# Transposes of a hybrid layer's mixer moved from TensorE to VectorE and DRAM stores

## The chip, the cores and the metric

One core of one Trainium2 chip runs the whole program in one launch. The metric is the device time of that core in microseconds. The kernel before was run three times: 2200.02, 2205.93 and 2200.26, median 2200.26 us. Engines are named as in the profile: PE is TensorE, DVE is VectorE, ACT is ScalarE, POOL is GpSimd, SP is SyncE, which issues nearly all DMA.

## What is computed

Two layers on a sequence of T = 1024 positions and D = 1024 channels, in float32. Layer 0 has a mixer of two parts that share one input projection, layer 1 a gated linear recurrence; a convolutional feed-forward network (FFN) follows each. The mixer of layer 0, cut to its core:

```python
def retention_deltanet_mixer(hn, pos, w_in, conv_w, a_log, dt_bias, out_gain, w_out):
    q_r, k_r, v_r, g_r, q_d, k_d, v_d, g_d, b_d, a_d = jnp.split(hn @ w_in, split_at, axis=-1)
    ...
    y_r = _rms(retention_chunkwise(q_r, k_r, v_r)).reshape(b, t, RET_WIDTH)
    y_r = y_r * jax.nn.silu(g_r.astype(f32))
    qkv = jax.nn.silu(causal_dwconv(jnp.concatenate([q_d, k_d, v_d], axis=-1), conv_w)).astype(f32)
    ...
    q_d = l2norm(q_d.reshape(b, t, GDN_HEADS, GDN_DK))
    k_d = l2norm(k_d.reshape(b, t, GDN_HEADS, GDN_DK))
    ...
    y_d = gated_delta_chunkwise(q_d, k_d, v_d, g, beta)
    y_d = rms_norm(y_d, out_gain) * jax.nn.silu(g_d.astype(f32).reshape(b, t, GDN_HEADS, GDN_DV))
    y = jnp.concatenate([y_r, y_d.reshape(b, t, GDN_WIDTH)], axis=-1).astype(hn.dtype)
    return y @ w_out
```

Both parts have four heads of 128 channels. Retention works on chunks of 128 positions: scores between q and k, a decaying state, and an RMS norm over the 128 channels of each position. The gated delta rule also solves a unit lower triangular system for each chunk, one for each head.

## The kernel before

**Layout.** Activations stand with channels on the 128 partitions and positions along the free axis. A projection of one head is a *unit*: weights of 1024 x 128, two quarters of 128 x 512. For each of the two halves of the sequence (512 positions) eight input tiles are multiplied into one PSUM bank. Float32 accuracy comes from splitting each operand in a high and a low part and doing three matmuls (`mm3`, L319 to L330): high by high, high by low, low by high. A half is therefore 24 matmuls of 128x512, and two halves rotate through a ring of four banks (`pp`); small products use four other banks (`pc`).

**Weights** are streamed in the order that `quarter_order` writes down: SP loads a raw quarter (L260), ACT casts its high part `whi` (L270), DVE subtracts for its low part `wlo` (L271). Six split quarters may be held at once.

**Order of the work.** `_mix0` projects, in turn, the gated-delta k heads (units 20 to 23), its q heads (16 to 19), four gates (12 to 15), its v heads (24 to 27), then for each retention head q, k and v (h, 4 + h, 8 + h) and a last gate. Beside the projections run *lanes*: lists of generators, of which one step is taken every second slot, a slot being one `mm3`. The lane of the gated delta rule holds the chunk matrices (`a_stage`), the triangular solve (`subst`: 31 steps of two DVE instructions, L1271 and L1273, on 32x32 blocks that 128 partitions hold), `merge` (which assembles 128x128 inverses out of blocks with short matmuls, L1305 to L1337), and eight `scan`s over chunks. The lane of retention holds two `ret_half` for each head. `after(n, f)` runs f n slots later, `flush` runs slots until nothing is left. A scheduler then fixes, for each engine, one order of instructions; an engine works through its own in that order and waits where an operand is not there.

**Transposes.** Scans and retention need v, K and k with positions on the partitions, and their outputs with channels on the partitions again. All of this is done by TensorE against an identity, into PSUM, four at a time: outputs in `post` (L1366, then an ACT copy, L1367, and one DMA to `y_dram`), v in `scan` (L1389), K in `scan` (L1397), v and k in `ret_half` (L1459, L1464). The squared norms of the q heads are sums over channels for each position: `qnorm` does them with eight matmuls against a column of ones (L1345), with positions on the partitions.

**Evacuations** from PSUM multiply by the row R of inverse norms (L388 for gates and heads). Gates go through `gate2` (L1105 on ACT, L1106 on DVE), convolved heads through `conv_tail` (L1203 and L1207 on ACT, L1205 and L1208 on DVE). In `a_stage`, L1235, L1236, L1231 and L1242 are DVE steps, L1246 the stores of blocks to `l_dram`; L1308 is one of merge's ACT copies; L1277 is the reordering copy at the solve's end; L1292 loads blocks of `t_dram` for merge.

**FFN.** Its down projection uses a product scheme with seven operands per group of channels. `store_parts` writes the hidden tiles to DRAM, some operands whole (`sf_dram`), some already split in high and low parts (`pf_dram`); `load_set` reads them back, and splits the whole ones on ACT and DVE (L840, L841).

Of the kernel before, what the change touches and what calls it, by code (L numbers as in the profile page):

```python
# [103 lines left out]
class Block:  # L104
# [82 lines left out]
    def quarter_order(self):  # L187
# [3 lines left out]
        for h in range(NH):  # L191
            o += [(("mix_in", i), 2) for i in (h, 4 + h, 8 + h)]
# [567 lines left out]
    def ffn(self, layer, gain):  # L760
# [3 lines left out]
        s_dram = self.tc.dram_tile([2, 4, 4, P, HALF], F32, name=f"sf_dram{layer}")  # L764
# [15 lines left out]
        place = {1: 0, 4: 1, 2: 2, 6: 3}  # L780
        whole = {0: 0, 1: 1, 3: 2, 5: 3}
        room = {}

        def store_parts(p, y, hi):
# [11 lines left out]
            def store_split(o, src, at):  # L796
                A.copy(halves(hi[:, at]), src)  # L797
                V.tensor_tensor(halves(lo[:, at]), src, f32(halves(hi[:, at])), ALU.subtract)
                for e, t in enumerate((hi, lo)):
                    nc.sync.dma_start(p_dram[c, whole[o], k % 4, e], f32(t[:, at]))  # L800
# [22 lines left out]
            store_split(5, v[:, :, 0], slice(HALF, T))  # L823

        def load_set(c, o):

            x = self.operand(o)
            if o in whole:
                for k in range(4):
                    for e in range(2):  # L830
                        nc.sync.dma_start(f32(x[:, :, 4 * e + k, :]), halves(p_dram[c, whole[o], k, e]))
# [120 lines left out]
    def rglru(self, gain):  # L952
# [5 lines left out]

        sm = lambda name: pool.tile([P, 8], F32, name=name)
# [12 lines left out]
        us = pool.tile([P, 8 * HALF], F32, name="us")  # L972
        xs = pool.tile([P, 4 * T], F32R, name="xs")
# [110 lines left out]
    def mix0(self, gain):  # L1084
        tc = self.tc
        self.q_dram = tc.dram_tile([NCH, P, HALF], F32, name="q_dram")
        self.v_dram = tc.dram_tile([NCH, P, HALF], F32, name="v_dram")
# [21 lines left out]
    def _mix0(self, room):  # L1109
# [89 lines left out]
        def conv_tail(kind, h, buf, dst):  # L1199
# [9 lines left out]
            return th  # L1209

# [131 lines left out]
        def qnorm(h, s):  # L1342
            p = self.pc()
            for n in range(NCH):
                PE.matmul(p[:, n:n + 1], s[:, n * P:(n + 1) * P], self.ones, start=True, stop=True)  # L1345

            V.tensor_scalar(irho[:, h * NCH:(h + 1) * NCH], p[:, 0:NCH], 4.0 * EPS, 128.0 * EPS, ALU.add, ALU.mult)

        def normalise(o, eps, ydst, i):
# [12 lines left out]

            def post():
                p = self.pc()
                for h in range(4):
                    PE.transpose(p[:, hs(h)], on[:, hs(h)], self.ident)  # L1366
                A.copy(s, p)  # L1367
                nc.sync.dma_start(ydst, ps4(s) if len(ydst.shape) == 3 else s)
            self.after(8, post)

        def scan(n):
# [4 lines left out]
            nc.sync.dma_start(v, self.v_dram[n])  # L1376
# [6 lines left out]
            yield from range(2)  # L1383
# [3 lines left out]
            pv = self.pc()  # L1387
            for h in range(NH):
                PE.transpose(pv[:, hs(h)], v[:, hs(h)], self.ident)  # L1389
# [3 lines left out]
            yield  # L1393
            if n < NCH - 1:
                p = self.pc()
                for h in range(NH):
                    PE.transpose(p[:, hs(h)], K[h][:, cs], self.ident)  # L1397
                kt = tmp2("kt")
                V.tensor_tensor(ps4(kt), ps4(p), bc_last(cn(ekt), P), ALU.mult)
            s0, s1 = S[n % 2], S[(n + 1) % 2]  # L1400
            if n > 0:
                p = self.pc()
                for h in range(NH):
                    PE.matmul(p[:, hs(h)], K[h][:, cs], s0[:, hs(h)], start=True, stop=True)
                for h in range(NH):
                    V.scalar_tensor_tensor(v[:, hs(h)], p[:, hs(h)], col(ck, h, n), v[:, hs(h)], ALU.mult, ALU.add)
# [22 lines left out]
            normalise(o, cn(irho), self.y_dram[4:8, :, cs].rearrange("h p c -> p h c"), 0)  # L1429


        def rot_head(ti):
# [3 lines left out]
            def evac(n, sl, ps):  # L1436
# [4 lines left out]
                G.tensor_tensor(r[:, sl], r[:, sl], t, ALU.add)  # L1441
            self.project(unit, evac)
# [266 lines left out]
```

## Time and profile before

| What | Value |
|---|---|
| median of three runs | 2200.26 us |
| the profiled execution | 2200.31 us |
| its span in the trace | 2198.5 us |
| PE busy | 2176.4 us (99%) |
| DVE busy | 1696.0 us (77%) |
| ACT busy | 1069.7 us (49%) |
| POOL busy | 80.8 us (4%) |

The span runs from the first to the last instruction of the trace; 1.8 us of the execution's time lie around it. A line of the trace gives a start, a duration, the engine, the line of the program, the operation and its operands by the program's names; in brackets stands the idle time of that engine just before, and what ended it. Matmuls are pipelined, so their durations overlap, and the distance of starts says what one costs. The mixer's projections and lanes take about the first 480 us.

### The profile page before, as it was taken

How to read it: one execution, taken by the hardware profiler on the slowest of the kernel's cores; microseconds unless marked ns; L12 is line 12 of the kernel's file. 1: busy time of each engine (PE TensorE's matmuls, PEld its weight loads, DVE VectorE, ACT ScalarE, POOL GpSimd, SP SyncE). 2: the span in 40 equal slices, each digit the busy share in tenths (PEclk: the TensorE clock that was granted, in tenths of full speed). 3: DMA queues.
4: the chain of work that ended last, by engine and by line, in shares of the span. 5: the costliest groups of instructions: out<-in, count | busy, mean ns of one | idle time of the engine just before them, and what ended most of it. 6: DMA issues, size and time to landing. Idle time of an engine off the chain costs nothing.

```text
span 2198.5 us, 29909 instructions
## 1 busy us (share of the span) xinstructions
PE 2176.4 (99%) x10844; PEld 1819.5 (83%) x10844; DVE 1696.0 (77%) x2576; ACT 1069.7 (49%) x1712; POOL 80.8 (4%) x73
## 2 busy tenths in 40 slices
PE   9999999999999999999999999999999999999998
PEld 8887888887888888887888888888888888878888
DVE  6988766446899988987865677778999889878644
ACT  5334433124565555554323476765655555544321
POOL 0100111200000000000000000000000000000001
PEclk9999999999999999999999999999999999999999
DMA  4243424125234544438546211242245445375542
GB/s 173 81 141 99 128 83 145 57 79 175 63 120 167 179 153 157 163 111 287 197 160 201 82 53 63 85 147 73 101 165 171 148 173 177 115 271 178 190 165 77
DMA packets 203300, 305.34 MB, mean 139 GB/s; under 512 B 31728, under 2 KB 91408, under 8 KB 203152
## 3 DMA queue, kind: packets, MB, share of 16 engines
q1 hardware_dynamic: 202720, 301.85, 40.7%
q8 instruction: 85, 1.39, 0.3%
q10 hardware_dynamic: 432, 1.58, 0.2%
q14 instruction: 63, 0.52, 0.1%
HBM read 212.63 MB, written 90.72 MB: 138 GB/s over the span
## 4 chain that ended last, share of the span: by engine, by line
PE 89%; DMA 4%; DVE 4%; issue 2%; ACT 1%; POOL 1%; SPq 0%; POOLq 0%; DVEq 0%; ACTq 0%
PE ps L328 27%; PE ps L330 27%; PE ps L329 27%; DMA t<-sf_dram 1%; DMA t<-y_dram 1%; PE pc L433 1%; DMA s<-pf_dram 1%; DMA h<-in_xT_dram 0%; DVE wlo L271 0%; PE pc L448 0%; DVE l L1273 0%; DVE l L1271 0%; PE pc L328 0%; PE pc L330 0%; PE pc L329 0%
## 5 line engine op out<-in xcount | busy, mean ns | idle before, releaser
L328 PE MATMUL ps<-s,whi 128*128 128x512 f32 (+1 forms) x2792 | 1091.0, 392 | 3.9 <-ACT s L840 1.8
L329 PE MATMUL ps<-s,whi 128*128 128x512 f32 (+1 forms) x2792 | 1084.5, 388 | 1.0 <-DVE s L841 0.7
L330 PE MATMUL ps<-s,wlo 128*128 128x512 f32 (+1 forms) x2792 | 1083.9, 388 | 0.0
L270 ACT CAST whi<-raw 128x512 fp32r<-128x512 f32 (+1 forms) x612 | 371.5, 613 | 659.1 <-PE ps L329 515.6
L328 PEld LDWEIGHTS ps<-s,whi 128*128 128x128 f32 x2792 | 524.9, 188 | 112.5 <-ACT s L840 3.1
L330 PEld LDWEIGHTS ps<-s,wlo 128*128 128x128 f32 x2792 | 524.7, 188 | 108.1 <-DVE wlo L271 0.3
L329 PEld LDWEIGHTS ps<-s,whi 128*128 128x128 f32 x2792 | 525.2, 188 | 107.3 <-DVE s L841 1.8
L271 DVE TENSOR_TENSOR wlo<-raw,whi 128x512 fp32r<-128x512 f32 (+1 forms) x612 | 412.9, 680 | 60.8 <-ACT whi L270 57.2
L774 DVE SCALAR_TENSOR_TENSOR t<-halo,cols,t 128x1024 f32<-128x1024 f32 x176 | 222.1, 1282 | 4.8 <-ACT t L772 3.5
L747 DVE TENSOR_TENSOR halo<-ps,kept 128x512 f32<-128x512 f32 (+1 forms) x138 | 92.2, 668 | 75.5 <-PE ps L330 74.2
L757 DVE TENSOR_TENSOR h<-ps,h 128x512 f32<-128x512 f32 x112 | 77.4, 691 | 82.2 <-PE ps L330 81.9
L772 ACT ACTIVATE t<-halo,cols 128x1024 f32<-128x1024 f32 x88 | 109.7, 1246 | 16.9 <-DVE halo L747 11.6
L742 ACT COPY kept<-ps 128x512 f32<-128x512 f32 (+1 forms) x138 | 77.0, 558 | 13.3 <-PE ps L330 11.2
L498 DVE TENSOR_TENSOR h<-ps,h 128x512 f32<-128x512 f32 (+1 forms) x72 | 45.3, 631 | 43.3 <-PE ps L330 43.3
L438 POOL TENSOR_TENSOR rtok<-rtok,npow 128x4 f32<-128x4 f32 (+1 forms) x11 | 11.2, 1016 | 1722.3 <-DVE rtok L437 1668.7
L857 DVE TENSOR_TENSOR t<-t 128x1024 f32<-128x1024 f32 x44 | 53.7, 1221 | 0.0
L797 ACT CAST t<-t 128x512 fp32r<-128x512 f32 x64 | 38.1, 620 | 32.0 <-DVE t L857 30.7
L852 ACT ACTIVATE t<-t 128x1024 f32<-128x1024 f32 x44 | 46.8, 1063 | 10.1 <-DVE t L774 10.0
L416 ACT ACTIVATE t<-h 128x512 f32<-128x512 f32 (+1 forms) x49 | 27.2, 562 | 46.3 <-DVE h L498 41.5
L840 ACT CAST s<-t 128x512 fp32r<-128x512 f32 x48 | 29.5, 621 | 38.4 <-DMA t<-sf_dram 34.0
L328 PE MATMUL ps<-s,s 128*128 128x256 f32 (+1 forms) x144 | 46.2, 321 | 0.0
L329 PE MATMUL ps<-s,s 128*128 128x256 f32 (+1 forms) x144 | 45.8, 318 | 0.0
(293 smaller groups left out, 2074.5 us busy)
## 6 DMA issues: line engine op xcount, KB each, us to landing
raw<-in_ffn_up_dram SPq DMA_DIRECT2D x176, 256.0 KB, 2.7
s<-pf_dram SPq DMA_DIRECT2D x128, 256.0 KB, 5.3
pf_dram<-t SPq DMA_DIRECT2D x64, 256.0 KB, 2.6
pf_dram<-lo SPq DMA_DIRECT2D x64, 256.0 KB, 2.5
sf_dram<-t SPq DMA_DIRECT2D x64, 256.0 KB, 2.2
t<-sf_dram SPq DMA_DIRECT2D x64, 256.0 KB, 5.0
raw<-in_ffn_w_dram SPq DMA_DIRECT2D x64, 256.0 KB, 2.9
raw<-in_mix_in_dram SPq DMA_DIRECT2D x62, 256.0 KB, 2.9
```

What stands on the lines that cost most here:

```text
L270: self.nc.scalar.copy(hi[:, 0:w], raw[:, 0:w])
L271: eng.tensor_tensor(lo[:, 0:w], raw[:, 0:w], f32(hi[:, 0:w]), ALU.subtract)
L328: mm(ps, whi, xhi, start=start, stop=False)
L329: mm(ps, whi, xlo, start=False, stop=False)
L330: mm(ps, wlo, xhi, start=False, stop=stop)
L742: A.copy(kept[o], ps)
L747: V.tensor_tensor(dst(i, j), v(ps), v(kept[k]), ALU.add)
L757: V.tensor_tensor(h(*to[o]), ps.rearrange("p (h c) -> p h c", c=256), h(*to[o]), ALU.add)
L772: A.activation(t, buf[:, 2:2 + T], AF.Identity, scale=w(0), bias=self.col(f"ffn_cb{layer}", tile_i))
L774: V.scalar_tensor_tensor(t, buf[:, 2 + j:2 + j + T], w(j), t, ALU.mult, ALU.add)
L852: A.activation(tg, tg, AF.Silu)
L857: V.tensor_tensor(tg, tg, tv, ALU.mult)
```

## The change

**Transposes.** None of the mixer's is left on TensorE. A new helper `store_t` does block transposes on DVE (each 32x32 block of a tile is transposed in its place) and stores the tile in DRAM with four DMAs that put the blocks in their places, in runs of 32 elements (128 bytes). So K goes to `kt_dram`, v to `v_dram`, the retention's k and v to `rt_dram`; scans and retention load them back with positions on the partitions. `post` transposes blocks on DVE and stores with 4 DMAs (scan) or 16 (retention) in the place of one.

**q norms.** Squares are block-transposed, reduced over 32 and block-transposed again on DVE, stored as rows to `qq_dram`, loaded back with positions on the partitions (elements of 4 bytes), and added on POOL.

**Leads.** Stores wait for three slots (`after(3)`), posts for six instead of eight; a scan loads its tiles four steps ahead of its first matmul instead of two; a retention half keeps four states in the place of two and does its state updates ahead of its output; the heads' units come as v, k, q instead of q, k, v.

**FFN.** Operand 5 of the first group is stored whole instead of split, and split on loading, in both layers. In the recurrence two tiles are allocated ahead of the small ones.

```diff
-            o += [(("mix_in", i), 2) for i in (h, 4 + h, 8 + h)]
+            o += [(("mix_in", i), 2) for i in (8 + h, 4 + h, h)]
...
-        place = {1: 0, 4: 1, 2: 2, 6: 3}
-        whole = {0: 0, 1: 1, 3: 2, 5: 3}
+        place = {1: 0, 4: 1, 2: 2, 6: 3, 5: 4}
+
+        whole = [{0: 0, 1: 1, 3: 2}, {0: 0, 1: 1, 3: 2, 5: 3}]
...
-            store_split(5, v[:, :, 0], slice(HALF, T))
+            if 5 in whole[c]:
+                store_split(5, v[:, :, 0], slice(HALF, T))
+            else:
+                nc.sync.dma_start(halves(s_dram[c, place[5], k % 4]), v[:, :, 0])
...
+        def store_t(dst, src, room):
+
+            V.transpose(room, src)
+
+            def out():
+                for a in range(4):
+                    bs = slice(a * 32, (a + 1) * 32)
+                    nc.sync.dma_start(dst[:, bs].rearrange("(b i) j -> i b j", i=32),
+                                      room[bs, :].rearrange("p (b j) -> p b j", j=32))
+            self.after(3, out)
...
-        def qnorm(h, s):
-            p = self.pc()
-            for n in range(NCH):
-                PE.matmul(p[:, n:n + 1], s[:, n * P:(n + 1) * P], self.ones, start=True, stop=True)
-
-            V.tensor_scalar(irho[:, h * NCH:(h + 1) * NCH], p[:, 0:NCH], 4.0 * EPS, 128.0 * EPS, ALU.add, ALU.mult)
+        def qnorm(h, s, room):
+            V.transpose(room, s)
+            V.tensor_reduce(qb, room.rearrange("p (b j) -> p b j", j=32), AX.X, ALU.add)
+            V.transpose(q32, qb)
+            d = self.qq_dram[h]
...
+            self.after(3, out)
+            self.after(8, load)
+            self.after(15, back)
...
             def post():
-                p = self.pc()
-                for h in range(4):
-                    PE.transpose(p[:, hs(h)], on[:, hs(h)], self.ident)
-                A.copy(s, p)
-                nc.sync.dma_start(ydst, ps4(s) if len(ydst.shape) == 3 else s)
-            self.after(8, post)
+                V.transpose(s, on)
+                for a in range(4):
+                    bs = slice(a * 32, (a + 1) * 32)
+                    for d, c in ydst(a):
+                        nc.sync.dma_start(d, s[bs, c].rearrange("p (m j) -> p m j", j=32))
+            self.after(6, post)
...
+            if n < NCH - 1:
+                kt = tmp2("kt")
+                nc.sync.dma_start(kt, self.kt_dram[cs])
...
-            yield from range(2)
+            yield from range(4)
...
-            pv = self.pc()
-            for h in range(NH):
-                PE.transpose(pv[:, hs(h)], v[:, hs(h)], self.ident)
-            V.tensor_tensor(ps4(v), ps4(pv), bc_last(cn(cv), P), ALU.mult)
+            V.tensor_tensor(ps4(v), ps4(v), bc_last(cn(cv), P), ALU.mult)
...
-            self.after(28, lambda h=h, q2=q2: qnorm(h, q2))
+            qnorm(h, q2, blocks())
+            store_t(self.kt_dram[:, hs(h)], K[h], blocks())
...
-            q = rot_head(h)
-            k = rot_head(4 + h)
...
-            self.project(unit, self.evac_r(v))
-            ret += [ret_half(h, i, q, k, v) for i in range(2)]
+            self.project(self.unit("mix_in", 8 + h), evac)
+            k = rot_head(4 + h, self.rt_dram[1, h])
+            q = rot_head(h)
+            ret_load(h)
+            ret += [ret_half(h, i, q, k) for i in range(2)]
```

The orders of the engines change well beyond the edited lines. On DVE before, at the start of the triangular solve (L1271 and L1273): wlo_1386 and wlo_1392 are the low parts of the first v head's weights (unit 24), ps_1301 and ps_1335 the second gate, ps_1396 the first half of the third gate.

```order
L1106 SCALAR_TENSOR_TENSOR t_1206<-t_1284,t_1206 128x1024
L271 TENSOR_TENSOR wlo_1386<-raw_1383,whi_1385 128x512
L388 TENSOR_TENSOR t_1300<-ps_1301,R_97 128x512
L388 TENSOR_TENSOR t_1300<-ps_1335,R_97 128x512
L1271 TENSOR_TENSOR l0_117<-l0_117 128x31
L271 TENSOR_TENSOR wlo_1392<-raw_1389,whi_1391 128x512
L1273 TENSOR_TENSOR l0_117<-l0_117 128x31
L1271 TENSOR_TENSOR l0_117<-l0_117 128x60
L1273 TENSOR_TENSOR l0_117<-l0_117 128x30x2
L1106 SCALAR_TENSOR_TENSOR t_1300<-t_1379,t_1300 128x1024
```

On DVE in the changed kernel, at the start of the solve (now L1291 and L1293): ps_1516 and ps_1550 are the two halves of the fourth and last gate.

```order
L388 TENSOR_TENSOR t_1515<-ps_1516,R_97 128x512
L388 TENSOR_TENSOR t_1515<-ps_1550,R_97 128x512
L1291 TENSOR_TENSOR l0_120<-l0_120 128x31
L1293 TENSOR_TENSOR l0_120<-l0_120 128x31
L1291 TENSOR_TENSOR l0_120<-l0_120 128x60
L1293 TENSOR_TENSOR l0_120<-l0_120 128x30x2
L1291 TENSOR_TENSOR l0_120<-l0_120 128x87
L1293 TENSOR_TENSOR l0_120<-l0_120 128x29x3
```

And on DVE in the changed kernel, where the first block of the solve ends after its twentieth step: wlo_1421 and wlo_1427 are the low parts of unit 24, wlo_1506 the first of unit 25.

```order
L1291 TENSOR_TENSOR l0_120<-l0_120 128x240
L1293 TENSOR_TENSOR l0_120<-l0_120 128x12x20
L1114 SCALAR_TENSOR_TENSOR t_1515<-t_1584,t_1515 128x1024
L271 TENSOR_TENSOR wlo_1421<-raw_1418,whi_1420 128x512
L271 TENSOR_TENSOR wlo_1427<-raw_1424,whi_1426 128x512
L1291 TENSOR_TENSOR l0_120<-l0_120 128x231
L1293 TENSOR_TENSOR l0_120<-l0_120 128x11x21
L1291 TENSOR_TENSOR l0_120<-l0_120 128x220
L271 TENSOR_TENSOR wlo_1506<-raw_1503,whi_1505 128x512
```

The solve moved from behind the second gate to behind the fourth, and the low parts of unit 24 from its first steps to behind its twentieth.

On PE in the changed kernel, where the last gate (ps_1550) ends and unit 24 (ps_1600, ps_1631) begins:

```order
L328 MATMUL ps_1550<-s1_96,whi_1341 128x512
L329 MATMUL ps_1550<-s1_96,whi_1341 128x512
L330 MATMUL ps_1550<-s1_96,wlo_1342 128x512
L328 MATMUL ps_1600<-s1_96,whi_1420 128x512
L329 MATMUL ps_1600<-s1_96,whi_1420 128x512
L328 MATMUL ps_1631<-s1_96,whi_1420 128x512
L330 MATMUL ps_1600<-s1_96,wlo_1421 128x512
L328 MATMUL ps_1600<-s1_96,whi_1420 128x512
```

Unit 24 follows the last gate with nothing between them, and three of its matmuls stand ahead of the first that needs a low part.

On PE in the changed kernel, the last head's merge (L1325 to L1357) and the first scan (L1428 to L1462):

```order
L1334 MATMUL pc_2307<-l0_120 32x32 x7
L1338 MATMUL pc_2308<-l0_120 32x32 x7
L1351 MATMUL pc_2331<-l0_120,h7_95 64x64 x3
L1351 MATMUL pc_2337<-l0_120,h7_95 64x64 x4
L1357 MATMUL pc_2343<-l0_120 64x64 x4
L1357 MATMUL pc_2350<-l0_120 64x64 x4
L1428 MATMUL pc_2487<-l0_120,h0_88 128x128
L1428 MATMUL pc_2487<-l0_120,h1_89 128x128
L1428 MATMUL pc_2487<-l0_120,h2_90 128x128
L1428 MATMUL pc_2487<-l0_120,h3_91 128x128
L1444 MATMUL pc_2502<-l0_120,h4_92 128x128
```

They stand behind each other without wide matmuls between.

On SP in the changed kernel, the stores of the last K head (kt_dram), the load of the solve's blocks (l_dram) and the raw weights of units 24 and 25:

```order
L1266 DMA l_dram_113<-h7_95 32x4x32 x8
L1371 DMA qq_dram_110<-l0_120 128x32
L1227 DMA kt_dram_108<-lo_1235 32x32x32
L1281 DMA l0_120<-l_dram_113 128x1024
L1227 DMA kt_dram_108<-lo_1235 32x32x32 x3
L1375 DMA l0_120<-qq_dram_110 128x8x1 x4
L1616 DMA g_dram_116<-t_1345 128x1024
L260 DMA raw_1418<-in_mix_in_dram 128x512
L260 DMA raw_1424<-in_mix_in_dram 128x512
```

Before, the first raw quarter of unit 24 (raw_1383) stood ahead of all stores to `l_dram`.

More of the change, by code (lines that the diff above doesn't have):

```diff
@@ L763, in ffn @@
         y_dram = self.tc.dram_tile([16, P, T], F32, name=f"yf_dram{layer}")
[L764 removed]
+        s_dram = self.tc.dram_tile([2, 5, 4, P, HALF], F32, name=f"sf_dram{layer}")
         p_dram = self.tc.dram_tile([2, 4, 4, 2, P, HALF], F32, name=f"pf_dram{layer}")
@@ L1456, in ret_half @@
             yield
[L1457 to L1466 removed]
+            vt, kt = rt[i]
+            A.activation(kt, kt, AF.Copy, scale=ktail[:, h:h + 1])
             yield
@@ L1494, in together @@
                 yield from range(2)
+        blocks = lambda: f32(self.parts.tile([P, T], F32R, tag="lo", name="lo"))
+        half = lambda: self.kept.tile([P, HALF], F32, tag="kept", name="kept")
         gdn = self.lane("gdn", 2, 0)
```

113 lines of the change are left out of this document (66 added, 47 removed).

## The prediction

> **What bounds the kernel now.** I read the busy table first, then the chain that ended last, then the table of stretches, and last the rows of the stretch that the change rewrites.
>
> ```profile
> PE 2176.4 (99%) x10844; PEld 1819.5 (83%) x10844; DVE 1696.0 (77%) x2576; ACT 1069.7 (49%) x1712; POOL 80.8 (4%) x73
> PE 89%; DMA 4%; DVE 4%; issue 2%; ACT 1%; POOL 1%; SPq 0%; POOLq 0%; DVEq 0%; ACTq 0%
> ```
>
> TensorE is busy nearly all the time and carries the chain, so a microsecond of TensorE work that disappears is worth a microsecond, as long as the other engines keep up. Whether they do is read by stretch. The columns below are length, then PE, weight load, DVE, ACT and POOL with counts, granted clock, DMA share and GB/s.
>
> ```profile
> 100.00:150.00 50.00, 50.00 (x270) 43.02 (x269) 41.66 (x105) 21.16 (x41) 8.64 (x4) 1.00 0.47 132
> 150.00:200.00 50.00, 49.74 (x274) 40.01 (x272) 45.51 (x95) 15.30 (x23) 0.00 (x0) 1.00 0.36 118
> 240.00:300.00 60.00, 59.79 (x400) 52.84 (x400) 41.54 (x81) 22.89 (x58) 10.73 (x8) 1.00 0.35 101
> 300.00:360.00 60.00, 57.57 (x386) 51.09 (x385) 42.87 (x90) 21.74 (x53) 14.78 (x12) 1.00 0.32 95
> ```
>
> From 100 to 200 us (gated-delta q heads, gates, v heads) VectorE is 83% and 91% busy beside a full TensorE: it has little room. In the scans (240 to 360 us) it is 69% to 71% busy. The next rows show how VectorE stands against TensorE before 200 us: evacuations of projections (L388) and rows of the triangular solve (L1271, L1273).
>
> ```profile
> 140.04 0.69 DVE L388 TENSOR_TENSOR t<-ps,R 128x512 f32<-128x512 f32 x1
> 149.40 0.20 DVE L1271 TENSOR_TENSOR l<-l 128x31 f32<-128x31 f32 x1
> 152.45 0.69 DVE L388 TENSOR_TENSOR t<-ps,R 128x512 f32<-128x512 f32 x1 [0.31 <-PE ps L330]
> 165.12 0.42 DVE L1271 TENSOR_TENSOR l<-l 128x255 f32<-128x255 f32 x1
> 165.58 0.42 DVE L1273 TENSOR_TENSOR l<-l 128x255 f32<-128x255 f32 x1
> 169.15 0.69 DVE L388 TENSOR_TENSOR t<-ps,R 128x512 f32<-128x512 f32 x1
> 180.23 0.69 DVE L388 TENSOR_TENSOR halo<-ps,R 128x512 f32<-128x512 f32 x1
> 162.00 0.39 PE L329 MATMUL ps<-s,whi 128*128 128x512 f32 x1
> 162.22 0.39 PE L330 MATMUL ps<-s,wlo 128*128 128x512 f32 x1
> 162.45 0.39 PE L328 MATMUL ps<-s,whi 128*128 128x512 f32 x1
> ```
>
> I name units g0 to g3 (mix_in 12 to 15, the gates), v0 to v3 (24 to 27) and their halves a and b. Matmuls start 0.22 to 0.23 us apart (162.00, 162.22, 162.45), 0.227 as I take it, so a half of 24 takes 5.44 us. The row at 152.45 waited for TensorE: it evacuates g2a, which so ran from 147.0 to 152.4. g3b ended 16.3 us later, at about 168.8 (evacuated at 169.15), v0b at about 179.6 (evacuated at 180.23). g0a was evacuated only at 140.04, 7 us before TensorE needed its bank again for g2a (the ring has four): VectorE runs late there, but not so late that TensorE waits. The solve's 31 steps run from 149.40 on, with the casts and evacuations of g2 to v1 between them.
>
> **The change part by part.** First the price of what leaves TensorE: the groups, the q norm in the chain, and one group of four transposes with its successor.
>
> ```profile
> L1366 PE MATMUL pc<-ident,l 128*128 128x128 f32 x64 | 9.6, 272 | 0.0
> L1459 PE MATMUL pc<-ident,t 128*128 128x128 f32 x32 | 4.8, 272 | 0.0
> L1464 PE MATMUL pc<-ident,t 128*128 128x128 f32 x32 | 4.8, 273 | 0.0
> L1389 PE MATMUL pc<-ident,l 128*128 128x128 f32 x32 | 4.8, 273 | 0.0
> L1397 PE MATMUL pc<-ident,h 128*128 128x128 f32 x28 | 4.2, 272 | 0.0
> 100.61 1.68 PE pc L1345 x16
> 144.67 1.68 PE pc L1345 x16
> 273.13 0.60 PE L1389 MATMUL pc<-ident,l 128*128 128x128 f32 x4
> 273.49 0.48 PE L328 MATMUL ps<-s,whi 128*128 128x512 f32 x1
> ```
>
> Busy time overlaps, so I price by starts: four transposes hold TensorE for 273.49 − 273.13 = 0.36 us, and the change back to wide matmuls costs 0.09 (0.48 against 0.39). With the 0.09 where nothing small stands beside them: 16 posts 16 × 0.45 = 7.2, scan v 8 × 0.36 = 2.9, scan K 7 × 0.36 = 2.5, retention v and k 8 × 0.81 = 6.5, together 19.1 us. The four q norms are 4 × (1.68 + 0.09) = 7.1 us. In all 26.2 us of TensorE work goes. Of this, 7.1 lies before 150 us, the rest behind 200 us.
>
> What VectorE gets has no row in this trace: 32x32 block transposes of 128x1024 and 128x512. The nearest rows are full-width operations and a reordering copy.
>
> ```profile
> L1208 DVE SCALAR_TENSOR_TENSOR t<-t 128x1024 f32<-128x1024 f32 x8 | 9.8, 1223 | 0.8 <-ACT t L1207 0.8
> L388 DVE TENSOR_TENSOR t<-ps,R 128x512 f32<-128x512 f32 x24 | 16.4, 688 | 13.1 <-PE ps L330 13.0
> 184.72 1.11 DVE L1277 COPY l<-l 128x1024 f32<-128x1024 f32 x1
> 103.19 1.12 DVE L1242 SCALAR_TENSOR_TENSOR h<-pc,l 128x128 f32<-128x128 f32 x4
> ```
>
> I take 1.2 us for 128x1024 and 0.65 for 128x512, and the same 1.2 for the new 128x1024 reduce; the ends I keep are 1.1 and 2.4 (half rate). [...]
>
> *q heads.* Per head a transpose, a reduce and the transpose of K come to VectorE, 3.6 us, plus 0.1. Three heads of this stand ahead of g0a's evacuation: 11.1 us. Of other work, 8 of the steps L1242 (four take 1.12, so 2.2) and two of L1231 (128x512, 0.6 each, as L388 by starts) now stand behind it, and one L1208 (1.1) ahead. Net +8.8 us, so g0a is evacuated at 140.04 + 8.8 = 148.8 if no idle time takes it up. TensorE would have reached g2a at 147.0 − 7.1 = 139.9; it now waits for that bank until 149.4. The 7.1 us of the q norms are lost in this, and g3b ends at 149.4 + 21.8 = 171.2 instead of 168.8.
>
> *The solve.* This is the term that decides. In the new VectorE order the first twenty steps, 40 instructions, stand in one block behind g3b's evacuation, and only then come L1114 and the low parts of v0's weights; before, v0's low parts stood in front of the second and third instruction of the solve. v0 follows g3 directly on TensorE and can do three matmuls without its low part.
>
> ```profile
> L1271 DVE TENSOR_TENSOR l<-l 128x31 f32<-128x31 f32 (+15 forms) x31 | 10.6, 341 | 0.7
> L1273 DVE TENSOR_TENSOR l<-l 128x31 f32<-128x31 f32 (+15 forms) x31 | 10.6, 342 | 0.8
> ```
>
> Their mean is 0.342 us at a mean width of 176 elements. The first twenty steps have a mean width of 192; from 0.20 at 31 and 0.42 at 255 an element is 0.001 us, so 0.36, and starts lie 0.04 further apart than the duration (165.58 − 165.12 = 0.46 against 0.42): 40 × 0.40 = 16.0 us. With the evacuation (0.6), L1114 (1.1) and one cast (0.6) TensorE waits 18.3 us, until 189.5. Of v0's 10.9 us three matmuls (0.7) are done, so v0 ends at 199.7 against 179.6: **+20.1 us**, the q norms' gain included.
>
> *Merges.* The triangular blocks are put together by short matmuls with ACT and VectorE between them:
>
> ```profile
> 235.89 0.26 ACT l L1308
> 237.02 0.35 ACT l L1321
> ```
>
> Before, wide matmuls stand between nearly all of them. In the new order the last head's merge and scan 0 stand without any behind each other, then wide matmuls whose low part is cast behind scan 0's VectorE work. Of five hops at 0.3 to 1 us each I estimate 5 us for that, and 4 for the three heads before, against the 3 they cost now: **+6** (0 to 10).
>
> *Scans and retention.* 19.1 us of TensorE work goes. VectorE gets 16 posts and 16 retention transposes, 32 × 0.65 = 20.8 us over 240 us: 5.2 more per 60, to 80%. ACT loses 16 copies of the posts, 8 of the retention's. I take 2 us of new waits: **−17.1**. The yields that move loads further ahead (four instead of two) hide DMA that does not stop TensorE now.
>
> *Queues.* The new stores and loads add about 280 DMA issues on SyncE, at 0.44 (the l_dram stores, 1.76 for four) to 0.54 us (the t_dram loads, 9.78 for 18) each and so 120 to 150 us, of which some 100 between 240 and 480 us: about half of that queue. Behind them stand weight loads.
>
> ```profile
> 99.13 1.76 SPq L1246 DMA_DIRECT2D l_dram<-h  x4
> 189.96 9.78 SPq L1292 DMA_DIRECT2D l<-t_dram  x18
> l<-t_dram SPq DMA_DIRECT2D x64, 16.0 KB, 1.9
> ```
>
> Transfers of 128-byte runs land in 1.9 us, and raw tiles are loaded ahead, so I take 0. POOL gets 12 tiny operations behind DMA waits; what it does next is needed late, 0.
>
> *FFN operand 5.* In each layer a load phase reads 1 MB less and splits 4 tiles more (each a cast on ACT and a subtraction on VectorE of 128x512).
>
> ```profile
> 1010.00:1050.00 40.00, 38.31 (x160) 29.04 (x159) 26.93 (x41) 17.25 (x29) 0.00 (x0) 1.00 0.92 325
> 1950.00:1990.00 40.00, 38.48 (x158) 30.27 (x157) 26.92 (x41) 17.10 (x29) 0.00 (x0) 0.96 0.90 320
> L840 ACT CAST s<-t 128x512 fp32r<-128x512 f32 x48 | 29.5, 621 | 38.4 <-DMA t<-sf_dram 34.0 <-PE ps L330 3.7
> 1039.17 0.50 PE L328 MATMUL ps<-s,whi 128*128 128x512 f32 x1 [0.55 <-ACT s L840]
> ```
>
> 160 matmuls at 0.227 are 36.3 us of 40: about 3.7 are lost where DMA is 0.92 busy. 1 MB at 325 GB/s is 3.2 us. ACT's splits (0.62 each) wait for the transfers, and TensorE for the splits, which become more, so I take half, **−3.5** for both layers (0 to −6.4).
>
> Sum: +20.1 + 6 − 17.1 − 3.5 = +5.5 us. The profiled run took 2200.31 us (span 2198.5 and 1.8 around it), 0.05 above the median, so the same sum holds: **2205.8 us**. A measurement of this kernel tells about 0.3%, 6.6 us, from no change. By its terms' ends this case reaches from 2194 (bank wait taken up by idle time, merges covered) to 2216.
>
> **The rivals.**
> *VectorE transposes at half rate* (slower). Six of them ahead of g0a and two ahead of g3 add 8 × 1.2 = 9.6 us on an engine that is already the late one; in the scans 20.8 us become 41.6, and VectorE stands at nearly 90%: 4 more. 2205.8 + 13.6 = 2219. It decides from about 1.9 us per 128x1024. The 1.11 us of the reordering copy speaks against it. [...]
>
> *SyncE late* (slower). A retention post now issues 16 stores, 16 × 0.44 = 7.0 us, ahead of a scan's loads and of weights. If two of the eight reach TensorE: 2219. The four yields speak against it.
>
> *Only the block, no lateness* (faster). If idle VectorE time takes up the transposes, g2a starts at 139.9, g3b ends at 161.7, v0 at 190.2: +10.6; with merges covered and no new waits, 10.6 − 19.1 − 3.5 = −12, 2188. For it: 8.3 us idle between 100 and 150. Against: that idle time lies in waits that stay.
>
> *TensorE stays the bound everywhere* (faster). The weights of v0 come in time after all: 2200.3 − 26.2 − 3.5 = 2171. The order speaks against it. That the change does not remove this work is excluded by the order: the transposes are gone from TensorE.
>
> **How the numbers follow.** Forecast 0.45 (0.02 of it faster, 0.24 same, 0.19 slower), half rate 0.17, SyncE 0.07, only the block 0.21 (0.04 same), TensorE-bound 0.10. Faster 0.02 + 0.17 + 0.10 = 0.29, same 0.28, slower 0.43. The range leaves out the TensorE-bound case and the far end of the slow ones: 2183 to 2224.
>
> **What would show it.** A TensorE wait of some 18 us behind g3, at 170 to 190 us, on a weight's low part; g0a's evacuation near 149; transposes of 1.2 us; 19 us less TensorE work between 200 and 480; the stretches of operand 5 shorter by 1 to 3 us. Without that long wait the forecast is wrong by its largest term; with transposes of 2 us the half-rate case holds.

## The result, and the profile after

The changed kernel takes **2256.28 us** (median of four runs, 2255.69 to 2260.15) against 2200.51 us: 1.0253 times as long, 95% interval 1.024 to 1.0266. The forecast of 2205.8 us and its range, up to 2224, were too low by 50 and 32 us.

The busy table and the chain by engine, of the changed kernel:

```profile
PE 2170.2 (96%) x10592; PEld 1806.1 (80%) x10592; DVE 1735.6 (77%) x2624; ACT 1054.2 (47%) x1688; POOL 82.0 (4%) x85
PE 85%; DVE 5%; DMA 3%; issue 2%; SPq 2%; ACT 1%; POOL 1%; DVEq 0%; POOLq 0%; ACTq 0%
```

TensorE's instructions fell by 252, as the change says, but its busy time only by 6 us, and 2% of the chain now lies in SyncE's issuing (by line: L1407, the posts' stores), which was 0%. The table of stretches, with the columns of the prediction:

```profile
100.00:150.00 50.00, 45.23 (x206) 37.25 (x205) 46.22 (x100) 19.04 (x35) 9.57 (x10) 0.93 0.46 80
150.00:200.00 50.00, 33.47 (x138) 26.78 (x137) 40.35 (x94) 10.62 (x20) 1.58 (x6) 0.83 0.67 174
240.00:300.00 60.00, 56.02 (x556) 43.77 (x555) 31.24 (x58) 15.55 (x36) 6.44 (x5) 0.94 0.29 59
300.00:360.00 60.00, 53.16 (x318) 46.27 (x317) 44.02 (x91) 18.55 (x48) 9.25 (x8) 0.92 0.57 145
360.00:420.00 60.00, 51.40 (x288) 44.38 (x286) 39.77 (x75) 15.57 (x39) 10.31 (x8) 0.91 0.52 123
420.00:480.00 60.00, 48.90 (x270) 41.55 (x271) 34.17 (x67) 11.28 (x23) 13.92 (x11) 0.94 0.43 93
480.00:540.00 60.00, 54.31 (x269) 44.78 (x267) 24.45 (x43) 6.67 (x10) 9.84 (x8) 1.00 0.48 133
540.00:600.00 60.00, 48.22 (x195) 37.47 (x196) 38.82 (x52) 23.75 (x41) 0.00 (x0) 0.89 0.62 202
```

TensorE idles in all of them: 4.8 us in the first, 16.5 in the second, then 4.0, 6.8, 8.6, 11.1, 5.7 and 11.8, together 69 us. VectorE is 81% busy in the second, but only 65% in the last and 57% in 420 to 480, where TensorE idles most after it. An average does not show what is short; what ended the waits tells more (total, times, longest):

```profile
PE ps L328 <- ACT whi L270: 33.3, 7, 13.4
PE ps L330 <- DVE wlo L271: 12.0, 5, 8.5
PE ps L328 <- DVE t L388: 4.7, 1, 4.7
```

Most is waiting for weights. First the stretch on which the prediction had its largest term, VectorE's and TensorE's rows of the changed kernel:

```profile
143.99 1.28 DVE L388 TENSOR_TENSOR t<-ps,R 128x512 f32<-128x512 f32 x2
168.87 0.69 DVE L388 TENSOR_TENSOR t<-ps,R 128x512 f32<-128x512 f32 x1 [2.81 <-PE ps L330]
169.48 0.20 DVE L1291 TENSOR_TENSOR l<-l 128x31 f32<-128x31 f32 x1
186.27 1.28 DVE L271 TENSOR_TENSOR wlo<-raw,whi 128x512 fp32r<-128x512 f32 x2
144.82 0.76 PE L328 MATMUL ps<-s,whi 128*128 128x512 f32 x1 [4.68 <-DVE t L388]
176.88 0.79 PE L328 MATMUL ps<-s,whi 128*128 128x512 f32 x1 [8.04 <-ACT whi L270]
187.01 0.80 PE L330 MATMUL ps<-s,wlo 128*128 128x512 f32 x1 [8.49 <-DVE wlo L271]
```

The gate's bank, the solve in one block from 169.48 on, the low part of v0 behind it at 186.27 and TensorE's start with it at 187.01: all as forecast, within 5 us. The 8.04 us for the high part, between them, were not. Most of the loss that was not forecast lies later. Rows of SyncE, ACT and TensorE around two of the longest waits:

```profile
449.62 0.70 DVE L1403 STREAM_TRANSPOSE l<-l 128x512 f32<-128x512 f32 x1
450.35 7.43 SPq L1407 DMA_DIRECT2D y_dram<-l  x16
457.82 0.91 SPq L260 DMA_DIRECT2D raw<-in_mix_in_dram  x2
460.98 1.25 ACT L270 CAST whi<-raw 128x512 fp32r<-128x512 f32 x2 [17.85 <-DMA raw<-in_mix_in_dram]
461.65 0.79 PE L328 MATMUL ps<-s,whi 128*128 128x512 f32 x1 [7.24 <-ACT whi L270]
536.58 0.71 DVE L1403 STREAM_TRANSPOSE l<-l 128x512 f32<-128x512 f32 x1
537.32 7.45 SPq L1407 DMA_DIRECT2D y_dram<-l  x16
545.34 0.85 SPq L260 DMA_DIRECT2D raw<-in_mix_in_dram  x2
550.30 0.80 PE L328 MATMUL ps<-s,whi 128*128 128x512 f32 x1 [13.35 <-ACT whi L270]
```

Read it from below: TensorE waits 13.35 us for weights; they were asked for at 545.34, behind the 16 stores of a post and one load, and the stores began when VectorE's transpose (536.58) was done. In SyncE's order the weights' loads stand behind the stores, so they were asked for only when the stores had waited and been issued. The same at 450 to 461.

### The profile page after: what moved, and what is told of

It reads as the page before. It is cut to its first block, busy times and chain, and to the rows that moved or that the text cites. A ratio compares the mean times of both kernels' runs of the same rounds, so it can differ in the third digit from the quotient of the medians.

```text
span 2255.1 us, 29794 instructions
## 1 busy us (share of the span) xinstructions
PE 2170.2 (96%) x10592; PEld 1806.1 (80%) x10592; DVE 1735.6 (77%) x2624; ACT 1054.2 (47%) x1688; POOL 82.0 (4%) x85
## 4 chain that ended last, share of the span: by engine, by line
PE 85%; DVE 5%; DMA 3%; issue 2%; SPq 2%; ACT 1%; POOL 1%; DVEq 0%; POOLq 0%; ACTq 0%
PE ps L328 27%; PE ps L330 27%; PE ps L329 26%; SPq L1407 2%; DMA t<-y_dram 1%; DMA h<-in_xT_dram 1%; PE pc L433 1%; DMA raw<-in_mix_in_dram 0%; PE pc L448 0%; DVE wlo L271 0%; DMA t<-sf_dram 0%; DVE l L1291 0%; PE pc L328 0%; PE pc L330 0%; PE pc L329 0%
## 5 line engine op out<-in xcount | busy, mean ns | idle before, releaser
L271 DVE TENSOR_TENSOR wlo<-raw,whi 128x512 fp32r<-128x512 f32 (+1 forms) x612 | 408.3, 674 | 46.1 <-ACT whi L270 44.0
L772 ACT ACTIVATE t<-halo,cols 128x1024 f32<-128x1024 f32 x88 | 109.7, 1246 | 16.1 <-DVE halo L747 11.1
L742 ACT COPY kept<-ps 128x512 f32<-128x512 f32 (+1 forms) x138 | 77.0, 558 | 13.4 <-PE ps L330 11.2
L844 ACT CAST s<-t 128x512 fp32r<-128x512 f32 x56 | 34.4, 621 | 30.9 <-DMA t<-sf_dram 26.3
```

The source lines that it names most:

```text
L271: eng.tensor_tensor(lo[:, 0:w], raw[:, 0:w], f32(hi[:, 0:w]), ALU.subtract)
L742: A.copy(kept[o], ps)
L772: A.activation(t, buf[:, 2:2 + T], AF.Identity, scale=w(0), bias=self.col(f"ffn_cb{layer}", tile_i))
```

## The experiments

Theory 1: weights stand in SyncE's queue behind stores. Theory 2: the lateness between the q heads is what costs. Each has the other as its rival, with VectorE's load as a third. Times are medians, but e1, e2, e3, e10 and e12 are of one run each; "before" beside them was 2199.4 to 2201.1 us. Runs of the kernel before in one batch lie up to 10 us apart (2197.4 to 2207.3), so a difference of 5 to 8 us that rests on a single run is not clear.

**e1, retention's posts through TensorE again.**

```diff
-            self.after(6, post)
+            self.after(8, post) if i == 1 else self.after(6, post_t)
```

Here `post` is the one of the kernel before, `post_t` the changed one.

> The changed kernel with one part undone: the eight posts of retention go through TensorE again and store once instead of 16 times; the eight posts of the scans stay on VectorE. Theory 1 (SyncE: weight loads stand in its queue behind posts' stores, which wait for VectorE and then take 7 us to issue): the waits for ACT's weight casts from 380 us on (1.2 + 7.2 + 2.1 + 13.4 us) and the slow matmuls behind them go, the posts cost 8 x 0.45 = 3.6 us of TensorE again: 2225 to 2235 us. Rival (the scans' waits come from VectorE, or are the lateness of 145 to 190 us carried on): under 6 us of change, 2250 to 2262.

Measured: 2234.07 us, 22 less. TensorE's waits for weight casts (the first line) fell by 23.7 us; posts on TensorE now wait for normalised outputs (the second):

```profile
PE ps L328 <- ACT whi L270: 9.6, 4, 7.1
PE pc L1405 <- DVE l L1399: 7.1, 6, 2.5
```

Within theory 1's range; the rival's is excluded.

**e2, all posts through TensorE.**

```diff
-            self.after(6, post)
+            self.after(8, post)
```

> The changed kernel with all 16 posts through TensorE again (one store each). Theory 1: the scans' posts have only 4 stores each, so beyond the run with retention's posts undone little is won, and 8 x 0.45 = 3.6 us of TensorE come back: 2225 to 2238. Rival (VectorE is what is short in the scans): VectorE loses 16 x 0.65 = 10 us, and the time falls by 8 to 12 more than with retention's posts alone.

Measured: 2226.14 us, 8 less than e1. This one cannot tell the theories apart: theory 1 expected 2225 to 2238, and the step from e1, 8 us, is the rival's, and both are single runs.

**e12, posts on VectorE with one store each**, decides between them (it leaves the blocks where the block transpose put them):

```diff
-                for a in range(4):
-                    bs = slice(a * 32, (a + 1) * 32)
-                    for d, c in ydst(a):
-                        nc.sync.dma_start(d, s[bs, c].rearrange("p (m j) -> p m j", j=32))
+                nc.sync.dma_start(ydst, ps4(s) if len(ydst.shape) == 3 else s)
```

> The changed kernel with the posts' transposes still on VectorE, but each post stored by one DMA, 512 bytes or more at a run, instead of 4 or 16 of 128-byte runs. It leaves out that blocks go to their transposed places. Theory 1 (the number of stores in SyncE's queue): TensorE's weight waits from 380 us on go as with the posts on TensorE, and 7.2 us of TensorE stay saved: 2218 to 2226. Rival (VectorE's share of the posts costs the time): 2240 to 2256.

Measured: 2217.66 us, 38.6 less than the changed kernel. VectorE does the same transposes, and in 420 to 480 us it is busier than in the changed kernel (37.56 against 34.17 us) while TensorE is full:

```profile
420.00:480.00 60.00, 60.00 (x304) 51.02 (x303) 37.56 (x63) 10.11 (x16) 18.07 (x14) 1.00 0.61 177
```

So the posts cost by their stores, not by VectorE. A store can cost by waiting at the head of SyncE's queue or by its issue. These are SyncE's waits for the transposed outputs, in the kernel before (240 to 480 us, where it waits for ACT's copy), the changed kernel (240 to 545) and e12 (240 to 500):

```profile
SPq L1368 <- ACT l L1367: 54.7, 16, 7.1
SPq L1407 <- DVE l L1403: 36.8, 8, 10.1
SPq L1404 <- DVE l L1403: 53.2, 11, 9.6
```

With the same stores' smaller entries it is 54.7, 55.7 and 65.7 us: they waited at the head as long before, and in e12 longer still. What the change adds is the issue: 160 stores hold SyncE for some 82 us, where 16 of 0.35 us held it for under 6. Slower transfers are not it either: the changed kernel's stores land in a median of 1.5 us (retention) or 1.9 us (scans), and a quarter of weights in 4.0 us there and in e12. The number of stores and the length of their runs were not tried apart.

**e3, q norms as before.**

```diff
-            qnorm(h, q2, blocks())
+            self.after(28, lambda h=h, q2=q2: qnorm(h, q2))
```

> The changed kernel with the q norms as before (eight matmuls against ones for each head). VectorE loses 4 x 2.5 us before 160 us and SyncE 20 DMAs. Theory (the lateness of VectorE by the transposes for the norms makes g2 wait and shifts the solve): the wait of 4.7 us for the gate's evacuation goes, the waits of 8.0 and 8.5 at the first v head shrink by half, 2 to 4 us of slow matmuls behind them go, 7.1 us of TensorE come back: 2243 to 2250. Rival (K's transposes and stores alone are enough for the lateness, since v0's raw weights stand behind them on SyncE): the waits stay and 7 us are added, 2256 to 2264.

Measured: 2251.13 us, 5 less. The waits at the gates and v0, 21.2 us, shrink to one of 5.63, and 7.1 us of matmuls come back; but weights are still waited for later, with a longest wait that grew:

```profile
175.23 0.79 PE L330 MATMUL ps<-s,wlo 128*128 128x512 f32 x1 [5.63 <-DVE wlo L271]
542.75 0.79 PE L328 MATMUL ps<-s,whi 128*128 128x512 f32 x1 [14.68 <-ACT whi L270]
```

Half of what the expectation had, 1 us above its range, and no more than a single run can show. Theory 2 is right for its place, and small for the whole.

**e16, the q norms as rows alone**, on the kernel before:

```diff
-            self.after(28, lambda h=h, q2=q2: qnorm(h, q2))
+            qnorm(h, q2, blocks())
```

> The kernel before with only the q norms as rows (VectorE, rows in DRAM, adds on GpSimd); nothing else of the change. TensorE loses 7.1 us. In the order the solve stands interleaved with weights, one gate later than before. Theory 5 (VectorE's 10 us more between the q heads make TensorE wait for gates' banks and the later merges lose their cover; the 7 us are given back): 2198 to 2206. Rival (the loss of the q stage came only with K's stores): the gain stays, 2193 to 2196.

Measured: 2207.14 us, 1.0025 of before (1.0015 to 1.0034), a loss although 7.1 us of TensorE went; it lies 1 us above theory 5's range. TensorE waits once for long:

```profile
136.10 0.76 PE L328 MATMUL ps<-s,whi 128*128 128x512 f32 x1 [5.05 <-DVE l L1239]
135.31 0.65 DVE L388 TENSOR_TENSOR halo<-ps,R 128x512 f32<-128x512 f32 x1
```

The profile names L1239, a tiny step that touches no PSUM bank; most likely the wait was for the evacuation of a projection's bank that ended just before it (the second row), which stood behind the norm's transpose (131.73) and reduce (133.47). That is theory 5's mechanism, one stage earlier than it said.

**e4, the FFN part alone** (the lines of the change, on the kernel before).

> The kernel before with only the FFN part: operand 5 of the first group stored whole and split on loading, in both layers. By the two traces TensorE's idle time in the two load phases falls from 1.7 and 1.5 us to 0.6 and 0.5: 2.1 us less, 2198. Rival (the extra splits cost what the smaller load gains): no change, 2200 to 2201. The prediction's term was -3.5: 2197.

Measured: 2199.5 us, ratio 0.9992 (0.9979 to 1.0005). A gain of 1 to 2 us is likely but not shown.

**e7, retention's part alone**, with the FFN part, on the kernel before (`store_t` for v and k, v, k, q, four states).

> The kernel before with only retention's part (v and k through VectorE and DRAM, v, k, q, four states, state updates ahead of the output) and the FFN part. TensorE loses 6.5 us of transposes. Theory 1 (only stores that stand ahead of weights and wait cost; rt_dram's 64 stores and 16 loads are issued between weights): a gain of part of it, 2193 to 2200. Rival (the loads of rt_dram hold back the weights): 2203 to 2215.

Measured: 2197.97 us, 0.9992 (0.9982 to 1.0003), in theory 1's range. The 6.5 us saved are mostly given back; its trace, of the slowest of its ten runs (2204.34 us), has four kinds of waits that before lacks or has smaller, of 2.9 to 3.9 us in all each (posts for outputs, a scan for v_dram among them). 64 more stores in that queue cost little here; they go four at a time, behind the transpose of an evacuation just made, which may be why.

**e17, the same with posts twelve slots behind** (`self.after(12, post)`); a retention half takes ten slots, so some of its outputs are overwritten before they are stored.

> The run with retention's and the FFN part alone (2198 us) with its posts, on TensorE there, twelve slots behind instead of eight. Of its trace 3.9 us of TensorE's waits end on VectorE's normalised outputs that posts wait for. If the lead is what they lack: 2193 to 2196, the fastest of the study. Rival (outputs come later to the output projection, which waits for them): 2198 to 2203.

Measured: 2201.88 us, 1.0003 (0.999 to 1.0015). No gain, within the rival's range. But the posts' wait for outputs grew, from 3.9 us in 3 waits to 10.3 in 11, which fits a post that now waits for the next half's output in the same tile. So the run does not tell whether the lead is what the posts lack.

**e8, v and K of the scans alone**, K behind the q heads as in the change, with the FFN part.

```diff
-        yield from range(2)
+        yield from range(4)
...
+            store_t(self.kt_dram[:, hs(h)], K[h], blocks())
...
+            store_t(self.v_dram[:, hs(h)], v, blocks())
```

> The kernel before with K transposed and stored behind the q heads (its place in the change), v behind the v heads, and the FFN part; q norms, posts and retention as before. Against the run with K behind the v heads it differs in K's place alone. Theory 2: in the order the first 13 steps of the solve stand in a block here, so TensorE waits 5 to 6 us on the first v head's low part and loses 2.8 us to slow matmuls: 8 us above that run. Rival (K's place does not matter without the norms): within 3 us of it.

Measured: 2222.46 us, 1.0089 (1.0073 to 1.0106): 23 us more than the FFN part alone. Its wait for the first v head's low part is there (6.2 us), as theory 2 said. **e6** has K's line behind the v heads instead; "the run before it" in its expectation is e5, below:

```diff
             store_t(self.v_dram[:, hs(h)], v, blocks())
+            store_t(self.kt_dram[:, hs(h)], K[h], blocks())
```

> As the run before it, and retention as before too (transposes on TensorE, q, k, v): of the change only v and K of the scans (through VectorE, behind the v heads), the four steps of lead and the FFN part are left. TensorE loses 2.9 + 2.5 us of transposes. Theory 1 and 2 (nothing stands ahead of weights or the solve): 2193 to 2197. Rival (a scan that must wait for three loads and stores of v and K late in SyncE's queue costs what it saves): 2199 to 2206.

Measured: 2226.56 us, 1.011 (1.0095 to 1.0125), 4 us more than e8, where theory 2 had 8 us less; it is far above both ranges. The solve does stand in its old place, and from 100 to 250 us nearly no wait is left (0.2 us), but the loss has another place, merge's loads:

```profile
PE pc L1325 <- DMA l<-t_dram: 12.4, 4, 6.3
250.00:300.00 50.00, 30.98 (x419) 25.61 (x418) 21.13 (x46) 17.76 (x43) 1.29 (x1) 0.64 0.50 115
```

In 250 to 300 us TensorE idles 19 us, at a granted clock of 0.64: the merges stand nearly alone there (35 of 419 matmuls are wide), behind the last v head. **e5**, the same with retention's part as well:

> All posts and the q norms on TensorE as before; K is transposed on VectorE and stored behind the v heads instead of behind the q heads, so nothing new stands on VectorE or SyncE before the solve, which has its interleaved place of the kernel before again; v, K and retention's v and k still go through VectorE and DRAM. Theory 2 (the waits of 4.7, 8.0 and 8.5 us and the slow matmuls behind them come from K and the norms between the q heads): against the run with all posts on TensorE (2226) these 21 us and 4 us of slow matmuls go, 7 us of norms come back: 2205 to 2212. Rival (the lateness is carried on by the loads that the later merges and scans wait for): 2215 to 2226.

Measured: 2229.38 us, 1.0123 (1.0107 to 1.0138): not theory 2, and 3 us above the rival's range.

**e9, e6 with merge's loads from GpSimd's queue.**

```diff
-                    nc.sync.dma_start(
+                    nc.gpsimd.dma_start(
                         ps4(w0s[key])[bs, :, bs],
```

> The run with v and K of the scans behind the v heads (2226.6 us), with one thing changed: merge's 64 loads of t_dram are issued from GpSimd's queue and not from SyncE's, where they stood behind v's and K's stores. Theory 3 (a queue is worked off in order; loads that are ready stand behind stores that are not, so the merges came after the last v head, without wide matmuls beside them): TensorE's waits for t_dram (12.4 us) and the slow matmuls of 250 to 300 us (clock 0.64) go: 2193 to 2203. Rival (VectorE's transposes of v and K, or the stores' DMA time, hold the merges and scans): 2215 to 2228.

Measured: 2233.0 us, 1.0144 (1.0127 to 1.0161), worse, a miss for theory 3 and above the rival's range too. The waits for t_dram are gone (one of 1.2 us is left), but the scans now start so late that little is left to cover them (27.7 us busy of 48 from 282 to 330). SyncE's rows of e9:

```profile
282.54 2.38 SPq L1227 DMA_DIRECT2D v_dram<-lo  x4
295.09 0.34 SPq L1397 DMA_DIRECT2D l<-v_dram  x1
298.30 2.30 SPq L1227 DMA_DIRECT2D kt_dram<-lo  x4
```

Eight transposes go through the single tile `lo`, so each has to wait for the stores of the one before; the last v is stored at 282.5, where the kernel before stored it at 233.7.

**e13, e6 with rooms of their own for the transposes.**

```diff
-            store_t(self.v_dram[:, hs(h)], v, blocks())
-            store_t(self.kt_dram[:, hs(h)], K[h], blocks())
+            store_t(self.v_dram[:, hs(h)], v, slots(14 + 4 * h % 6, 2))
+            store_t(self.kt_dram[:, hs(h)], K[h], slots(14 + (4 * h + 2) % 6, 2))
```

> The run with v and K of the scans behind the v heads (2226.6 us), with a room of their own for their transposes: three rooms in the solve's tiles in turn instead of the single tile lo, so that a transpose need not wait until the store before it (three slots later) has landed. Merge's loads stay on SyncE. Theory 4 (the single room strings the eight transposes and stores together): scans start earlier, 2195 to 2210. Rival, theory 3 alone (the loads of t_dram stand behind the stores in SyncE's queue): 2215 to 2228.

Measured: 2220.1 us, 1.0095 (1.008 to 1.011), in the rival's range. **e14** does both:

> The run before it with merge's loads from GpSimd's queue as well. Theories 3 and 4 together (merges late by the queue, scans late by the single room): neither is left, TensorE keeps the 5.4 us of transposes that v and K save: 2193 to 2200. Rival (the stores of 128-byte runs or VectorE hold the scans): over 2210.

Measured: 2206.59 us, 1.0032 (1.002 to 1.0044), between the two ranges. The rooms alone gain 6.5 us, the queue alone loses 6.4, the queue with the rooms gains 13.5 more: 20 of the 26 us that e6 lost. What is left in e14 is waits for VectorE in scans and retention (its largest: 7.6 us of posts for normalised outputs, 3.4 for a rotated head's evacuation). That it is VectorE's load was not tested.

**e15, e14 with retention's part.**

> The run before it with retention's part as in the change (v and k through VectorE and DRAM, 2198 us alone): the version that the runs so far point to, with q norms and posts on TensorE. If gains add up, 2 to 5 us under the run before it: 2188 to 2198. Rival (retention's stores in SyncE's queue and VectorE's load in the scans take it back): 2200 to 2215.

Measured: 2209.54 us, 1.0043 (1.0026 to 1.006), in the rival's range. The gains do not add up; no version of the study beats the kernel before beyond its interval.

**e10, the changed kernel with merge's loads from GpSimd's queue** (the edit of e9).

> The changed kernel with merge's 64 loads from GpSimd's queue, all else unchanged. Theory 3: the merges come between the v heads again and the last merge and scan 0 find wide matmuls beside them; the waits of 145 to 190 us and those behind retention's posts stay: 8 to 15 us less, 2241 to 2248. Rival (merges' place is worth nothing as long as the solve is late): 2252 to 2260.

Measured: 2243.19 us, 13 less: theory 3 holds in the changed kernel. The last of merge's loads there, behind v's last stores on SyncE, and in e10 on GpSimd (the third row):

```profile
265.41 2.23 SPq L1227 DMA_DIRECT2D v_dram<-lo  x4
271.42 8.26 SPq L1312 DMA_DIRECT2D l<-t_dram  x16
242.32 8.25 POOL L1312 DMA_DIRECT2D l<-t_dram  x14 [2.46 <-ACT l L1341]
```

**e11, all 128-byte stores from GpSimd's queue too.** The posts' line; those of `store_t`, cut in two by rows, and of merge are changed likewise:

```diff
-                        nc.sync.dma_start(d, s[bs, c].rearrange("p (m j) -> p m j", j=32))
+                        nc.gpsimd.dma_start(d, s[bs, c].rearrange("p (m j) -> p m j", j=32))
```

> The changed kernel with all 128-byte stores (store_t, in eights instead of fours, and posts) and merge's loads issued from GpSimd's queue; q norms' rows, weights and plain loads stay on SyncE. Nothing is taken from VectorE or from DMA. In the order the solve stands interleaved with weights again. Theory 3 for the whole loss: the 65 us of TensorE's idle time before 600 us and the slow matmuls behind it mostly go: 2180 to 2205. Rival (VectorE's and DMA's load cause the waits): over 2235. Between the two: GpSimd's own steps (the power in the norms) stand behind its stores now and hold the posts.

Measured: 2430.33 us, 1.1038 (1.1022 to 1.1055). GpSimd is far slower here as an issuer, of stores of 64 KB in 128-byte runs:

```profile
170.14 0.66 POOL L1229 DMA_DIRECT2D kt_dram<-lo  x1 [2.42 <-issue]
172.59 0.66 POOL L1229 DMA_DIRECT2D kt_dram<-lo  x1 [1.79 <-issue]
```

One each 2.45 us, where SyncE issues four of 128 KB in 2.3 to 2.4 us (e9's rows above). So the run says nothing of theory 1, only that this queue is no way out.

## Why the prediction was wrong, step by step

- **The prices on VectorE were right.** Groups of the changed kernel (x16 posts, x4 squares):

```profile
L1403 DVE STREAM_TRANSPOSE l<-l 128x512 f32<-128x512 f32 x16 | 11.3, 706 | 0.2
L1365 DVE STREAM_TRANSPOSE lo<-l 128x1024 f32<-128x1024 f32 x4 | 5.0, 1239 | 0.5 <-DMA kt_dram<-lo 0.5
```

  1.24 and 0.71 us against 1.2 and 0.65: the half-rate rival is out. 512 more elements for each partition take 0.53 us, as between L388 and L1208 of the prediction (0.69 and 1.22). Nor are VectorE's transposes of the posts what costs: e12 keeps them and takes 38.6 us less.
- **The q heads and the solve (+20.1) were right in size.** v0 was evacuated at 199.26 instead of 180.23, 19.0 us later. On the way errors cancelled, which is luck: g0a was evacuated at 143.99, not 148.8, so TensorE waited 4.7 us for its bank, not 9.5. From g3b's last matmul (evacuated from 168.87 on) to 187.01 are 18.3 us, as worked out. The first part of that wait was for the high part, asked for at 171 behind K's stores on SyncE, which the prediction had not seen, and the slow clock behind each wait (0.50) was not in it.
- **Merges (+6) were too small.** e10 shows 13 us for merge's loads alone. They stand behind v's stores in SyncE's queue, a cause that the prediction did not name; its own causes, missing cover and casts behind the scan, were not tried apart.
- **The step that failed: queues, "so I take 0".** Its two reasons were a landing time of 1.9 us and raw tiles loaded ahead. Neither is about the queue's order. Behind the wait for VectorE, which the one store before had as well, 16 stores take 7.4 us to issue, and the weights behind them are late by that. For the posts the stores cost 38.6 us (e12); with one store each the changed kernel takes 2217.7 us, inside the range. The prediction counted these issues, and half of the queue for them, and still took 0. The rival "SyncE late" had the mechanism and the 7 us right, but let only two posts of eight reach TensorE, at a chance of 0.07.
- **Scans and retention (−17.1)** came out as a loss, most of it by the posts' stores, some by merge's loads and the single room of v and K (e13, e14). By parts, with the FFN part and retention's at −3 us (e7), v and K +23 (e8), q norms +5 (e3), posts +30 (e2), the sum is +55, and +55.8 was measured. That these add up may be luck, since the parts use one queue, two of the four are single runs, and in e15 they do not add up.
- **FFN (−3.5)** measured −1.0 by the medians, with an interval that holds 0.
- **A term was missing: the clock.** Behind waits of 4.7 to 13.4 us TensorE ran at a granted clock of 0.50 for up to 4.9 us (the last section), which the prediction left out for every stall: at least 10 us in all.

## What to carry to other kernels

When a step gets more DMAs, read what stands behind them in the same queue, and price the issue of all of them against the next load that TensorE needs; a short landing time said nothing about it here (16 stores landed in a median of 1.5 us each and took 7.4 us to issue), and a queue that is half full by an average, as this one was by the prediction's count, may have no slack where a burst stands. Where a chain of steps shares one buffer, look at what its steps wait for: rooms of their own gained 6.5 us here (e13 against e6). Work taken off a full engine did not pay here, where the order that the scheduler then made moved weights and cover (26.2 us priced off TensorE, 55.8 us lost): look at the order first.

## What the runs showed of the hardware

Behind five waits of the changed kernel (4.68, 8.04, 8.49, 7.24 and 13.35 us, ending at 144.82, 176.88, 187.01, 461.65 and 550.30) TensorE's granted clock was 0.50. Rows behind the matmul at 144.82, which had waited 4.68 us, and the stretch ahead of it, with a granted clock (the third column from the right) of 0.50:

```profile
145.38 0.63 PE L329 MATMUL ps<-s,whi 128*128 128x512 f32 x1
145.81 0.63 PE L330 MATMUL ps<-s,wlo 128*128 128x512 f32 x1
149.15 0.39 PE L329 MATMUL ps<-s,whi 128*128 128x512 f32 x1
149.38 0.40 PE L330 MATMUL ps<-s,wlo 128*128 128x512 f32 x1
142.50:143.00 0.50, 0.00 (x0) 0.00 (x0) 0.50 (x3) 0.00 (x0) 0.00 (x0) 0.50 0.21 33
```

Starts are 0.43 us apart up to 149, then 0.23: ten matmuls lose 0.2 us each, so this wait of 4.7 us cost 6.7. Between 130 and 620 us the changed kernel has 51 such distances between wide matmuls, so it loses at least 10 us by them. The slow starts lasted 4.3 us from 144.82 on, 3.1 us from 187.01 (to 190.10) and 4.9 us from 550.30 (to 555.16). The fall, where the granted clock goes from 1.00 to 0.50, came at 142.2, 2.1 us after TensorE's last matmul had ended (140.14), and in the next long wait at 172.9, 4.1 us after (168.83).

In e13 the wide matmul at 289.09 was slow behind a wait of only 1.68 us, but the clock had fallen at 285.9 (by the mean of 0.98 in the first row), ahead of that wait, in a stretch of short matmuls with a wait of 1.95 us:

```profile
283.00:286.00 3.00, 1.05 (x20) 0.89 (x17) 1.84 (x5) 1.70 (x5) 0.00 (x0) 0.98 1.04 383
286.00:289.00 3.00, 1.25 (x10) 0.93 (x8) 1.43 (x3) 3.00 (x10) 0.00 (x0) 0.50 0.64 184
```

How sparse the work must be for the clock to fall was not tried.
